# Attention over all keys: the context's scores are taken earlier and turned in a score bank, three query-tile score sets are made ahead instead of five, and two query tiles are turned inside the first iteration

## The chip, the cores and the metric

One Trainium2 chip, one core of it. Its engines are PE (TensorE: matrix products and transposes; its weight loads are PEld), DVE (VectorE), ACT (ScalarE), POOL (GpSimd) and SP (SyncE, which only issues transfers here). Each has its own queue of instructions and runs it in order; they wait for each other through semaphores. PE writes into eight PSUM banks, which ACT and DVE empty.

The metric is the device time of one execution in microseconds (us), the median of several; less is better. The kernel before takes 1534.35 us (three runs, 1534.03 to 1535.56).

## What is computed

Two layers of a diffusion backbone over 1024 latent tokens and 128 context tokens, 1024 features wide. The change lies in one part of layer 0, the grouped-query attention: 8 query heads share 2 key heads of 64 features. Cut to what matters:

```python
def block_attend(q, k, v):                       # q (B,KV,G,T,D); k, v (B,KV,S,D)
    s = einsum('bkgqd,bksd->bkgqs', qi, k) * scale
    p = softmax(s, axis=-1)
    return einsum('bkgqs,bksd->bkgqd', p, v)

qb = rmsnorm(to_heads(qb, HQ_B), g_q)            # then axial rope
k_all = concatenate([kb_pos, kv_ctx[0]], axis=2) # 1024 latent + 128 cached keys
hb = block_attend(qb, k_all, v_all)              # latent queries
```

The 128 context tokens attend to themselves alone, with the same heads; that is a small separate attention. What follows is `y = concat(ha, hb) * silu(z)` and the output projection.

## The kernel before

Tokens are nine tiles of 128 (0 to 7 latent, 8 context). A float32 operand is cut into a high and a low part, so that each product is two or three matmuls.

**Phase g** makes keys, values and queries. `gqa_q` (L848) runs twice, for the first and the last four query heads (g = 0, 1). For each tile i it multiplies the normalised input by the weights (`tok`, L381 to L383: 24 matmuls of 256 columns into a bank of the pair "pj"), applies norm and rope on ACT, DVE and POOL (`norm_rope`, tile nr), turns the result with two PE transposes (L106) into the bank "tr" (even i) or "ptr" (odd i), and cuts the turned tile into Q: for each half of the partitions ACT casts the high part (L875) and DVE subtracts it (L876). In the program the second half's cast waits for the first half's subtraction.

In the second run some **score sets** are made ahead (`early`): a set is one query tile with one pair of heads against the 1152 keys, in six score groups. A group is two matmuls of 384 columns (L907) into one of three banks "s", which DVE copies out with the running extreme (L908). After three groups (one head) ACT takes the exponential over 1152 columns (L914), DVE the reciprocal (L915), POOL the division in three pieces (L917). The order of all engines in phase g is made by a scheduler with estimated times.

**Phase gqa** (`gqa`, L955) works off 32 sets, two at a time: j is the pair of heads (0 to 3), i = 0, 2, 4, 6 the query tile pair. One iteration holds ten **turn steps** n = 0 to 9 (`gqa_turn`, L922), each with four PE transposes of probabilities (two in steps 4 and 9) into the banks tr, pj, ptr, pj in rotation, emptied into the tiles pt by ACT (L938), in steps 4 and 9 by DVE (L936). Between them stand the score groups of the next two sets, one after each step and two ahead (`steps`); then the **apply**, 36 matmuls of 256 columns (L947) into bank "o". PE's order here is that of the code (`manual_schedule`); the other engines follow the scheduler.

In iteration i = 6 of each j the **context tile** is attended to as well (`ctx_steps`, L1014): four small score matmuls (L1023) into two s banks, DVE's maximum (L1024), two exponentials on ACT (L1027), sum and reciprocal on DVE (L1028, L1029), division on POOL (L1030); then two transposes of the result into bank "tr" (L106, tr<-pt) and their copy; after the apply the product with the values (L1042).

For j >= 2 each iteration also cuts one block of the output weights: a transfer into a buffer "raw", ACT's high part (L114), POOL's low part wlo (L115). The **output projection** follows (L381 to L383 with yh, yl). Its tile 0 is loaded by SP (y<-yd) into a buffer raw that the last weight block has left, and is cut by ACT (yh) and DVE (yl).

Of the kernel before, what the change touches and what calls it, by code (L numbers as in the profile page):

```python
# [10 lines left out]
F32 = mybir.dt.float32  # L11
F32R = mybir.dt.float32r
AF = mybir.ActivationFunctionType
ALU = mybir.AluOpType
# [4 lines left out]
P = 128  # L19
# [7 lines left out]
DHB = 64  # L27
# [12 lines left out]
class Kern:  # L40
    def __init__(self, ctx, tc, a, dbg):
        self.tc, self.nc, self.a, self.dbg = tc, tc.nc, a, dbg
        mk = lambda n, **k: ctx.enter_context(tc.tile_pool(name=n, bufs=1, **k))
        self.cp = mk("const")
        self.up = mk("slots")
        self.wp = mk("stage")
        self.sp = mk("small")
        self.dp = mk("scratch", space=DRAM)
        self.pp = mk("psum", space=PSUM)
        self.uid = 0  # L50
        self.flip = 0
        self.turn = 0

    @contextmanager
    def phase(self, n, *tags):
# [794 lines left out]
    def gqa_q(self, h, g, w, Qs, early):  # L850

        nc = self.nc
        ahead = None
        rhs = lambda k: tuple(x[:, (k % 4) * 256 : (k % 4 + 1) * 256] for x in w[k // 4])
        Q = []
        for i in range(NT):
            if i == NT - 4:
                ahead = self.gqa_weights(2) if g == 0 else self.gqa_gate(0)
            if i in (0, 2, 4, 6, 8) and g:
                n = len(early)  # L860
                q0 = Qs[0][n // 2][:, n % 2]
                early.append([])
                for _ in self.gqa_scores([q0[:, hh] for hh in range(2)], 0, lambda s: self.u(s, n="pr"), early[-1]):
                    pass
            ps = self.tok(h, i, rhs, 256)
            q = self.norm_rope(ps, 4, 0, i)
            pt = self.ps(("tr", "ptr")[i % 2])[:, :256]
            for j in range(2):
                self.flipped(pt[:, j * P : (j + 1) * P], q[:, 2 * j : 2 * j + 2].rearrange("p a b -> p (a b)"))
            if i % 2 == 0:  # L870
                Q.append(self.u([P, 2, 4, P], F32R, n="Q"))
            for hh in range(2):
                x = pt[hh * DHB : (hh + 1) * DHB].rearrange("p (a b) -> p a b", b=P)
                hi, lo = (Q[-1][r * DHB : (r + 1) * DHB, i % 2, hh::2, :] for r in (g, 1 - g))
                nc.scalar.copy(hi, x)  # L875
                nc.vector.tensor_tensor(lo, x, hi.bitcast(F32), ALU.subtract)  # L876
        return Q, ahead

    def zb(self, h):
# [74 lines left out]
    def gqa(self, Q, gz, early, between):  # L954

        kv = lambda j: j // 2
        V = lambda t, j: t[..., kv(j) * DHB : (kv(j) + 1) * DHB]
        q = lambda j, i: [Q[kv(j)][i // 2][:, i % 2, 2 * (j % 2) + hh, :] for hh in range(2)]  # L960
        place = (lambda s: self.t("pr", 4, s)), (lambda s: self.u(s, n="pr"))
        todo = iter([(j, i) for j in range(4) for i in range(8)])

        def tiles(out):
            for j, i in itertools.islice(todo, 2):
                if early:
                    out.append(early.pop(0))
                else:
                    prs = []
                    yield from self.gqa_scores(q(j, i), kv(j), place[i % 2], prs)  # L970
                    out.append(prs)

        prs, banks = [], ("tr", "pj", "ptr", "pj")
        for _ in tiles(prs):
            pass
        for j in range(4):
            y = self.ytile()
            for i in range(0, 8, 2):
                if i % 4 == 0:
                    po = self.ps("o")  # L980
                nxt, pts = [], ([], [])
                steps = tiles(nxt)
                turns = self.gqa_turn(prs, pts, banks)
                if i == 6:
                    ctx = self.ctx_steps([self.gqa_terms(x, kv(j), [self.KstP[:, b] for b in range(4)]) for x in q(j, 8)], [V(self.VP, j)] * 2, self.pt)
                next(steps, None)
                next(steps, None)
                for n, _ in enumerate(turns):
                    if i == 6 and n == 1:
                        next(ctx)  # L990
                    else:
                        next(steps, None)
                    if i == 6 and n == 6:
                        next(ctx)
                for _ in steps:
                    pass
                self.gqa_apply(pts, V(self.V, j), po[:, i % 4 * P : (i % 4 + 2) * P])
                if i == 6:
                    cpo = next(ctx)
                prs = nxt  # L1000
                if j >= 2:
                    next(between, None)
                if i % 4:
                    self.put_y(4 + j, slice((i - 2) * P, (i + 2) * P), po, gz, y)
            self.put_y(4 + j, slice(8 * P, NT * P), cpo, gz, y)
            gz = self.gqa_gate(j + 1) if j < 3 else None
        return y
# [624 lines left out]
```

## Time and profile before

| | |
|---|---|
| median of three runs | 1534.35 us |
| the profiled execution, its own time | 1537.54 us |
| its span, first to last instruction | 1535.8 us |
| PE busy | 1493.2 us, 97% |
| DVE, ACT, POOL busy | 54%, 46%, 29% |
| mean granted clock of PE over the span | 0.995 |

A timeline row has the start, the time of one instruction or a run of equal ones, engine, line, what is written from what, the count, and in brackets the idle time ahead with what ended it. A row of waits says which engine and line waited for which, with total time, number of waits and the longest. [...]

### The profile page before, as it was taken

The numbers are of one execution on the slowest core, as the hardware profiler recorded it, in microseconds if no ns is written. First come the engines' busy times: TensorE is split into PE (matmuls) and PEld (weight loads), VectorE is DVE, ScalarE is ACT, GpSimd is POOL, SyncE is SP. The second block draws the span as 40 slices with busy tenths as digits, with TensorE's granted clock in tenths as the row PEclk, the third lists the DMA queues.
The fourth block names the chain that finished last, engine by engine and source line by source line (L and its number), as shares of the span: only waits on it lengthen the run. The fifth ranks groups of instructions, "written<-read, shape, count | busy, mean of one in ns | idle before, by whom it ended". The sixth has DMA issues, their size and how long they took to land.

```text
span 1535.8 us, 27072 instructions
## 1 busy us (share of the span) xinstructions
PE 1493.2 (97%) x10139; PEld 1375.7 (90%) x10139; DVE 825.7 (54%) x2387; ACT 712.5 (46%) x1767; POOL 448.6 (29%) x644
## 2 busy tenths in 40 slices
PE   7899999999999899999999999999999999999998
PEld 5799999999999888877888989999999999988786
DVE  5832888863468666665565352535344434445532
ACT  4533535262446667776444352535344434345411
POOL 0001202011146645675223241323133222233200
PEclk9999999999999999999999999999999999999999
DMA  9203447332310000112334222131213122125342
GB/s 378 76 15 140 179 146 248 125 121 75 111 48 29 16 32 24 44 64 68 135 114 138 70 65 74 36 106 34 85 38 103 32 79 71 54 90 163 106 132 82
DMA packets 73283, 143.80 MB, mean 94 GB/s; under 512 B 15736, under 2 KB 44608, under 8 KB 73152
## 3 DMA queue, kind: packets, MB, share of 16 engines
q1 hardware_dynamic: 68566, 126.91, 24.7%
q10 hardware_dynamic: 4586, 15.16, 2.7%
q8 instruction: 80, 1.31, 0.3%
q14 instruction: 51, 0.42, 0.1%
HBM read 115.47 MB, written 21.86 MB: 89 GB/s over the span
## 4 chain that ended last, share of the span: by engine, by line
PE 49%; DMA 1%; DVE 1%; ACT 1%; POOL 1%; issue 1%; DVEq 0%; POOLq 0%
PE pj L366 7%; PE pj L367 7%; PE pj L368 7%; PE pj L382 6%; PE pj L381 6%; PE pj L383 6%; PE o L1282 4%; PE s L1259 3%; PE ptr L106 2%; PE tr L106 2%; DMA y<-yd 1%; DMA raw<-in_w_out_dram 1%; POOL wlo L115 0%; PE o L947 0%; DVE sb L1265 0%
## 5 line engine op out<-in xcount | busy, mean ns | idle before, releaser
L366 PE MATMUL pj<-hh,whi 128*128 128x384 f32 x1168 | 400.2, 343 | 1.9 <-ACT qT L101 1.2
L367 PE MATMUL pj<-hl,whi 128*128 128x384 f32 x1168 | 397.0, 340 | 0.0
L368 PE MATMUL pj<-hh,wlo 128*128 128x384 f32 x1168 | 395.6, 339 | 0.4 <-DVE wlo L115 0.4
L366 PEld LDWEIGHTS pj<-hh,whi 128*128 128x128 f32 x1168 | 219.6, 188 | 5.6 <-ACT qT L101 1.8
L368 PEld LDWEIGHTS pj<-hh,wlo 128*128 128x128 f32 x1168 | 219.3, 188 | 1.6 <-DVE wlo L115 0.6
L367 PEld LDWEIGHTS pj<-hl,whi 128*128 128x128 f32 x1168 | 219.8, 188 | 1.1
L1269 POOL TENSOR_SCALAR sb<-sb,sm 128x512 f32<-128x512 f32 (+1 forms) x128 | 84.7, 667 | 249.3 <-DVE sm L1268 237.6
L115 POOL TENSOR_TENSOR wlo<-raw,whi 128x1024 fp32r<-128x1024 f32 x43 | 103.0, 2400 | 133.0 <-ACT whi L114 115.7
L917 POOL TENSOR_SCALAR pr<-pr,smg 128x384 f32<-128x384 f32 x192 | 109.3, 586 | 80.5 <-PE pj L106 41.2
L381 PE MATMUL pj<-whi,hh 128*128 128x256 f32 x432 | 122.6, 285 | 0.3 <-DVE nr L782 0.3
L382 PE MATMUL pj<-wlo,hh 128*128 128x256 f32 x432 | 122.7, 284 | 0.0
L383 PE MATMUL pj<-whi,hl 128*128 128x256 f32 x432 | 122.4, 284 | 0.0
L908 DVE CUSTOM_DVE_ANT_0 pr<-s,zero 128x384 f32<-128x384 f32 x192 | 103.4, 553 | 24.9 <-PE s L907 21.4
L381 PE MATMUL pj<-whi,yh 128*128 128x512 f32 x288 | 114.2, 396 | 1.5 <-DVE o L1077 1.5
L382 PE MATMUL pj<-wlo,yh 128*128 128x512 f32 x288 | 113.7, 395 | 0.0
L383 PE MATMUL pj<-whi,yl 128*128 128x512 f32 x288 | 113.3, 394 | 0.0
L1267 ACT ACTIVATE sb<-sb,sm 128x512 f32<-128x512 f32 (+1 forms) x128 | 88.9, 695 | 52.7 <-DVE sm L1265 48.8
L907 PE MATMUL s<-Kst,Q 128*128 128x384 f32 x384 | 107.6, 372 | 0.7 <-DVE smg L908 0.7
L253 DVE CUSTOM_DVE_ANT_0 mj<-wm,cb 128x512 f32<-128x512 f32 x128 | 89.3, 697 | 5.1 <-DMA wm<-in_w_modT_dram 2.8
L114 ACT CAST whi<-raw 128x1024 fp32r<-128x1024 f32 x77 | 79.7, 1045 | 19.9 <-DMA raw<-in_w_v_dram 6.9
L1265 DVE CUSTOM_DVE_ANT_1 sb<-s,bias 128x512 f32<-128x512 f32 (+1 forms) x112 | 72.9, 664 | 24.9 <-PE ptr L106 12.6
L381 PEld LDWEIGHTS pj<-whi,hh 128*128 128x128 f32 x432 | 81.3, 188 | 1.3 <-issue 0.5
(346 smaller groups left out, 2908.8 us busy)
## 6 DMA issues: line engine op xcount, KB each, us to landing
wm<-in_w_modT_dram SPq DMA_DIRECT2D x32, 512.0 KB, 4.8
raw<-in_w_c_dram SPq DMA_DIRECT2D x25, 512.0 KB, 3.6
raw<-in_w_ab_dram SPq DMA_DIRECT2D x20, 512.0 KB, 3.5
e<-rbd ACTq DMA_DIRECT2D x12, 768.0 KB, 7.4
bias<-in_na_bias_dram SPq DMA_DIRECT2D x16, 576.0 KB, 4.1
wm<-in_w_mod_dram SPq DMA_DIRECT2D x16, 512.0 KB, 9.8
raw<-in_w_out_dram SPq DMA_DIRECT2D x16, 512.0 KB, 3.5
y<-yd SPq DMA_DIRECT2D x18, 448.0 KB, 3.4
```

The source lines that it names most:

```text
L115: (eng_lo or nc.gpsimd).tensor_tensor(lo, src, hi.bitcast(F32), ALU.subtract)
L253: nc.vector.tensor_tensor_reduce(junk, w[:, b, :], cb[:, r, :], 1.0, 0.0, ALU.mult, ALU.add, mp[:, hf, q // 4, 2 * (q % 4) + b, r : r + 1])
L366: nc.tensor.matmul(ps[:, :CW], a, hh, start=k == 0, stop=False)
L367: nc.tensor.matmul(ps[:, :CW], a, hl, start=False, stop=False)
L368: nc.tensor.matmul(ps[:, :CW], b, hh, start=False, stop=k == KB - 1)
L381: nc.tensor.matmul(ps[:, :width], hh, a, start=k == 0, stop=False)
L382: nc.tensor.matmul(ps[:, :width], hh, b, start=False, stop=False)
L383: nc.tensor.matmul(ps[:, :width], hl, a, start=False, stop=k == KB - 1)
L907: nc.tensor.matmul(s[:, :CW], x, y, start=part == 0, stop=part == 1)
L908: nc.vector.tensor_tensor_reduce(pr[:, c, :], s[:, :CW], zero, -1.0, -NEG, ALU.add, ALU.min, m3[:, c : c + 1])
L917: nc.gpsimd.tensor_scalar(pr[:, c, :], pr[:, c, :], r, 0.5, ALU.mult, ALU.mult)
L1267: nc.scalar.activation(x, x, AF.Exp, bias=nm, scale=-1.0, accum_out=r)
```

## The change

Three edits. First, the sets made ahead in phase g are three instead of five, at tiles 1, 3 and 5. Second, in the second run of `gqa_q` the turning of tiles 7 and 8 is put off: it is kept as a function, called in the first iteration of phase gqa behind turn steps 5 and 7. Third, the context tile's scores are put into iteration i = 4 behind step 7, in the place of a score group; its transposes come behind step 5 of iteration i = 6, ahead of the group there, and go to an s bank instead of tr.

```diff
-            if i in (0, 2, 4, 6, 8) and g:
+            if i in (1, 3, 5) and g:
...
-            pt = self.ps(("tr", "ptr")[i % 2])[:, :256]
...
+            def turned(i=i, q=q, Qt=Q[-1]):
+                pt = self.ps(("tr", "ptr")[i % 2])[:, :256]
...
+            if g and i in (7, 8):
+                self.turned.append(turned)
+            else:
+                turned()
...
-                if i == 6:
-                    ctx = self.ctx_steps([self.gqa_terms(x, kv(j), [self.KstP[:, b] for b in range(4)]) for x in q(j, 8)], [V(self.VP, j)] * 2, self.pt)
+                if i == 4:
+                    ctx = self.ctx_steps([self.gqa_terms(x, kv(j), [self.KstP[:, b] for b in range(4)]) for x in q(j, 8)], [V(self.VP, j)] * 2, self.pt, banks=("s", "s"))
...
-                    if i == 6 and n == 1:
+                    if (j, i, n) in ((0, 0, 5), (0, 0, 7)):
+                        self.turned.pop(0)()
+                    if i == 4 and n == 7 or i == 6 and n == 5:
                         next(ctx)
-                    else:
+                    if (i, n) != (4, 7):
                         next(steps, None)
-                    if i == 6 and n == 6:
-                        next(ctx)
```

Eight lines are added ahead, so that L106 becomes L107, L875 L878, L907 L915, L914 L922, L938 L946, L947 L955, L1023 L1031 and L1030 L1038.

**Place 1, the seam of phases g and gqa.** PE before, from the turning of tile 7 (nr_5712) to that of tile 8 (nr_5802) and the first turn steps (pr into ptr, pj); the s rows are the last sets made ahead:

```order
L106 MATMUL ptr_5726<-cc,nr_5712 128x128 x2
L907 MATMUL s_5757<-Kst_4302,Q_4980 128x384
L907 MATMUL s_5757<-Kst_4304,Q_4980 128x384
L907 MATMUL s_5761<-Kst_4302,Q_4980 128x384
L907 MATMUL s_5761<-Kst_4304,Q_4980 128x384
L907 MATMUL s_5765<-Kst_4302,Q_4980 128x384
L907 MATMUL s_5765<-Kst_4304,Q_4980 128x384
L106 MATMUL tr_5816<-cc,nr_5802 128x128 x2
L106 MATMUL ptr_5845<-cc,pr_5183 128x128
L106 MATMUL ptr_5845<-cc,pr_5320 128x128
L106 MATMUL ptr_5845<-cc,pr_5183 128x128
```

Now tiles 7 (nr_5668) and 8 (nr_5707) stand among the turn steps 5 to 8 of the first iteration; PE:

```order
L107 MATMUL ptr_5809<-cc,pr_5389 128x128
L107 MATMUL ptr_5815<-cc,nr_5668 128x128 x2
L107 MATMUL pj_5822<-cc,pr_5252 128x128
L107 MATMUL pj_5822<-cc,pr_5389 128x128
L107 MATMUL pj_5822<-cc,pr_5252 128x128
L107 MATMUL pj_5822<-cc,pr_5389 128x128
L107 MATMUL tr_5828<-cc,pr_5252 128x128
L107 MATMUL tr_5828<-cc,pr_5389 128x128
L107 MATMUL tr_5828<-cc,pr_5252 128x128
L107 MATMUL tr_5828<-cc,pr_5389 128x128
L107 MATMUL tr_5834<-cc,nr_5707 128x128 x2
```

Tile 7 goes into the bank ptr right behind a turn step that filled it, tile 8 into tr likewise. ACT there, from the second exponential of set 2 (pr_5528) to the copy that frees tr for tile 8:

```order
L922 ACTIVATE pr_5528,smg_5544<-pr_5528,smg_5542 128x1152
L946 COPY pt_5726<-pj_5747 128x512
L878 CAST Q_5635<-tr_5636 64x2x128
L946 COPY pt_5726<-ptr_5765 128x512
L922 ACTIVATE pr_5737,smg_5759<-pr_5737,smg_5757 128x1152
L946 COPY pt_5727<-pj_5777 128x512
L946 COPY pt_5727<-tr_5787 128x512
L946 COPY pt_5728<-ptr_5809 128x512
L922 ACTIVATE pr_5771,smg_5799<-pr_5771,smg_5797 128x1152
L878 CAST Q_5635<-ptr_5815 64x2x128
L946 COPY pt_5729<-pj_5822 128x512
L946 COPY pt_5729<-tr_5828 128x512
```

Two exponentials of the set now made in this iteration (pr_5737, pr_5771) have come in between the copies.

**Place 2, the context tile of j = 0.** PE before, in iteration 6 from a score group to the turning of the context's probabilities (pt_5830) and on:

```order
L907 MATMUL s_6301<-Kst_4302,Q_4794 128x384
L907 MATMUL s_6301<-Kst_4304,Q_4794 128x384
L106 MATMUL tr_6305<-cc,pt_5830 128x128 x2
L106 MATMUL ptr_6309<-cc,pr_6068 128x128
L106 MATMUL ptr_6309<-cc,pr_6146 128x128
```

Now PE has the context's scores in the end of iteration 4 (KstP is the context's keys):

```order
L107 MATMUL tr_6140<-cc,pr_5981 128x128
L1031 MATMUL s_6147<-KstP,Q_5175 128x128 x2
L1031 MATMUL s_6151<-KstP,Q_5175 128x128 x2
L107 MATMUL pj_6161<-cc,pr_5903 128x128
L107 MATMUL pj_6161<-cc,pr_5981 128x128
L107 MATMUL pj_6161<-cc,pr_5903 128x128
L107 MATMUL pj_6161<-cc,pr_5981 128x128
L915 MATMUL s_6169<-Kst_4302,Q_5082 128x384
L915 MATMUL s_6169<-Kst_4304,Q_5082 128x384
L107 MATMUL ptr_6173<-cc,pr_5903 128x128
L107 MATMUL ptr_6173<-cc,pr_5981 128x128
L915 MATMUL s_6177<-Kst_4302,Q_5082 128x384
```

The scores have moved up by most of an iteration; the third score group behind them (s_6177) waits in the program for the first of the context's two exponentials.

**Place 3, the end of the phase.** POOL before, from the division of the last set but one to the context's division (L1030):

```order
L917 TENSOR_SCALAR pr_8184<-pr_8184,smg_8212 128x384 x3
L115 TENSOR_TENSOR wlo_8277<-raw_8274,whi_8276 128x1024
L917 TENSOR_SCALAR pr_8224<-pr_8224,smg_8250 128x384 x3
L115 TENSOR_TENSOR wlo_8379<-raw_8376,whi_8378 128x1024
L1030 TENSOR_TENSOR pt_5830<-pt_5830,sm_8301 128x256
```

POOL now:

```order
L925 TENSOR_SCALAR pr_8184<-pr_8184,smg_8212 128x384 x3
L1038 TENSOR_TENSOR pt_5726<-pt_5726,sm_8233 128x256
L116 TENSOR_TENSOR wlo_8292<-raw_8289,whi_8291 128x1024
L925 TENSOR_SCALAR pr_8245<-pr_8245,smg_8265 128x384 x3
L116 TENSOR_TENSOR wlo_8379<-raw_8376,whi_8378 128x1024
```

The context's division stands ahead of the last two weight blocks instead of behind them.

## Rows read from the trace of the kernel before

**Rows 1.** The page: busy time, share of the span, instructions.
```profile
PE 1493.2 (97%) x10139; PEld 1375.7 (90%) x10139; DVE 825.7 (54%) x2387; ACT 712.5 (46%) x1767; POOL 448.6 (29%) x644
```

**Rows 2.** Waits of PE from 400 to 720 us: total, times, longest.
```profile
PE tr L106 <- POOL pt L1030: 6.2, 4, 2.2
PE ptr L106 <- DVE Q L876: 1.9, 1, 1.9
PE tr L106 <- DVE Q L876: 0.9, 1, 0.9
...
PE s L907 <- DVE smg L908: 0.7, 1, 0.7
```

**Rows 3.** Timeline of PE at the seam of phases g and gqa.
```profile
514.61 0.28 PE L383 MATMUL pj<-whi,hl 128*128 128x256 f32 x1
...
519.51 0.44 PE L106 MATMUL tr<-cc,nr 128*128 128x128 f32 x2 [0.50 <-POOL nr L784]
521.87 1.09 PE L106 MATMUL ptr<-cc,pr 128*128 128x128 f32 x4 [1.92 <-DVE Q L876]
...
528.90 4.11 PE L947 MATMUL o<-pt,V 128*64 128x256 f32 x36
```

**Rows 4.** Windows there: length; busy PE, PEld, DVE, ACT, POOL; granted clock; DMA.
```profile
520.00:521.00 1.00, 0.00 (x0) 0.00 (x0) 1.00 (x5) 0.97 (x2) 1.00 (x3) 0.96 0.00 0
521.00:522.00 1.00, 0.13 (x1) 0.16 (x2) 0.91 (x5) 0.95 (x4) 0.14 (x1) 0.50 0.00 0
...
527.00:528.00 1.00, 1.00 (x8) 1.00 (x7) 0.00 (x0) 0.67 (x2) 0.00 (x0) 0.63 0.00 0
```

**Rows 5.** Timeline of PE in the next two iterations.
```profile
539.27 4.20 PE L947 MATMUL o<-pt,V 128*64 128x256 f32 x36
...
551.77 4.11 PE L947 MATMUL o<-pt,V 128*64 128x256 f32 x36
```

**Rows 6.** Timeline of ACT in iteration 4 of j = 0.
```profile
549.12 1.26 ACT L914 ACTIVATE pr<-pr,smg 128x1152 f32<-128x1152 f32 x1
...
550.37 0.57 ACT L938 COPY pt<-pj 128x512 f32<-128x512 f32 x1
550.84 0.60 ACT L938 COPY pt<-tr 128x512 f32<-128x512 f32 x1
```

**Rows 7.** Groups of ACT by line and shape, 455 to 730 us: busy, mean ns.
```profile
L775 ACT ACTIVATE nr<-pj 128x64 f32<-128x64 f32 x68 | 14.4, 221 | 9.6 <-PE pj L383 8.5 <-POOL sm L134 0.9
...
L875 ACT CAST Q<-ptr 64x256 fp32r<-64x256 f32 x16 | 5.9, 367 | 4.5 <-DVE Q L876 2.4 <-PE ptr L106 1.9
...
L1027 ACT ACTIVATE pt<-s,sm 128x128 f32<-128x128 f32 x8 | 2.9, 363 | 0.0
```

**Rows 8.** Timeline of PE at the end of phase gqa.
```profile
711.85 0.66 PE L106 MATMUL pj<-cc,pr 128*128 128x128 f32 x4
...
717.74 0.44 PE L106 MATMUL tr<-cc,pt 128*128 128x128 f32 x2 [2.20 <-POOL pt L1030]
...
719.44 5.50 PE L947 MATMUL o<-pt,V 128*64 128x256 f32 x36
...
725.09 0.50 PE L381 MATMUL pj<-whi,yh 128*128 128x512 f32 x1
```

**Rows 9.** Timeline of POOL there.
```profile
709.02 1.71 POOL L917 TENSOR_SCALAR pr<-pr,smg 128x384 f32<-128x384 f32 x3 [0.43 <-DVE smg L912]
...
714.72 2.40 POOL L115 TENSOR_TENSOR wlo<-raw,whi 128x1024 fp32r<-128x1024 f32 x1
717.09 0.60 POOL L1030 TENSOR_TENSOR pt<-pt,sm 128x256 f32<-128x256 f32 x1
```

**Rows 10.** Timeline of SP's queue there.
```profile
717.14 0.38 SPq L1056 DMA_DIRECT2D y<-yd  x1
```

**Rows 11.** Timeline of ACT there.
```profile
720.71 0.94 ACT L114 CAST yh<-y 128x896 fp32r<-128x896 f32 x1 [0.93 <-DMA y<-yd]
```

**Rows 12.** Window there, columns as in rows 4.
```profile
718.00:719.00 1.00, 1.00 (x11) 1.00 (x10) 0.42 (x1) 0.29 (x1) 0.00 (x0) 0.94 0.58 145
```

More of the change, by code (lines that the diff above doesn't have):

```diff
@@ L52, in __init__ @@
         self.turn = 0
+        self.turned = []
     @contextmanager
@@ L866, in gqa_q @@
             q = self.norm_rope(ps, 4, 0, i)
-            pt = self.ps(("tr", "ptr")[i % 2])[:, :256]
-            for j in range(2):
-                self.flipped(pt[:, j * P : (j + 1) * P], q[:, 2 * j : 2 * j + 2].rearrange("p a b -> p (a b)"))
             if i % 2 == 0:
                 Q.append(self.u([P, 2, 4, P], F32R, n="Q"))
[L872 to L876, printed above, removed]
+            def turned(i=i, q=q, Qt=Q[-1]):
+                pt = self.ps(("tr", "ptr")[i % 2])[:, :256]
+                for j in range(2):
+                    self.flipped(pt[:, j * P : (j + 1) * P], q[:, 2 * j : 2 * j + 2].rearrange("p a b -> p (a b)"))
+                for hh in range(2):
+                    x = pt[hh * DHB : (hh + 1) * DHB].rearrange("p (a b) -> p a b", b=P)
+                    hi, lo = (Qt[r * DHB : (r + 1) * DHB, i % 2, hh::2, :] for r in (g, 1 - g))
+                    nc.scalar.copy(hi, x)
+                    nc.vector.tensor_tensor(lo, x, hi.bitcast(F32), ALU.subtract)
+            if g and i in (7, 8):
+                self.turned.append(turned)
+            else:
+                turned()
         return Q, ahead
```

## The prediction

> **What bounds the kernel now.** I read the page's busy times first: PE is busy for 97% of the span [rows 1], so only PE's queue sets the end. A moved instruction can save no PE work; it can save idle time of PE or time at the half clock. The list of PE's waits is read next, over the stretch that the change touches, 400 to 720 us [rows 2]. The largest item is the context's transposes waiting for POOL's division (L1030): 6.2 us in four waits, one for each pair of heads, the longest 2.2, so 4.0 in the other three. Three smaller ones (1.9 and 0.9 on DVE's low part of Q, 0.7 on the score copies) lie in one place, the seam between phases g and gqa.
>
> Then the timelines of these places. At the seam PE has the last projection matmul at 514.61 (T0 from here) and the first apply at 528.90 [rows 3]: 14.3 us. [...] At the end of gqa the wait of 2.20 ends at 717.74 [rows 8], the clock leaves the full level in 718 to 719 [rows 12], and the apply there takes 5.50 [rows 8] instead of the 4.11 of the first one [rows 3]. An apply during a low clock thus costs 1.4 us more.
>
> Times below are made against the profiled execution, 1537.54 us with a span of 1535.8 (1.7 around it); it is 3.2 above the median of 1534.35. The gain is taken over to the median.
>
> **1. Six score groups moved from phase g into iteration 2.** Six of the early groups go. Iteration 2 of j = 0 goes from 6 groups to 12. From the end of the first apply (528.90 + 4.11) to the second (539.27) are 6.3 us with six groups; from that apply's end (543.47) to the third (551.77) are 8.3 with twelve [rows 3, 5]. So a group costs PE 0.34 us, and six cost 2.0 here and save 2.0 in phase g, where they also filled PE's time. I take 0. Were they covering waits of PE on norm and rope, as much as those 2.0 would be lost; nothing excludes a gain of the size of the 0.7 on the score copies [rows 2].
>
> **2. The seam.** The work between T0 and the apply is the same on PE: six groups, ten turn steps, three turnings of Q. At full speed that is 6.3 us (iteration 2 has the same ten steps and six groups) plus three turnings of at most 0.44 [rows 3], 7.6. So the gain is at most 14.3 - 7.6 = 6.7, and the waits decide. The waits of 1.92 and 0.86 on Q's low parts go: tile 8 no longer stands ahead of the turn steps. What is late next is ACT, because two exponentials of the set that is now made here stand between its copies. By the new order ACT has, from T0 to the copy that frees tr for tile 8: four squares at 0.22, three Q casts at 0.37 [rows 7], three exponentials at 1.25 with the reading of the sum and seven copies at 0.47 [rows 6]: 0.9 + 1.1 + 3.75 + 3.3 = 9.05. With 0.4 before the first (T0's matmul must end) and 0.5 for exponentials that wait for DVE's minimum, T0 + 9.9. Tile 7 goes into bank ptr right behind a turn step that filled it, and so waits for the copy of that step: about 1.4 us on PE. Tile 8 in tr waits likewise, about 1.6, until T0 + 10. Queued behind each of them on PE are all later turn steps and the apply. Then tile 8, two turn steps and the last group, 1.1: apply at T0 + 11.1, against 14.3: 3.2 gained at full clock.
>
> The clock takes part of it back. Before, it fell after the 0.50 and inside the 1.92 [rows 3, 4]; now two waits of 1.4 and 1.6 stand within about four us, and I take it that it falls behind them. It then hits the apply, 1.4 by [rows 3, 8], and about 0.4 of turn steps. Net 1.4. The bounds are 0 (ACT and the clock eat all) and 6.7.
>
> [...]
> [...]
>
> **3. The context tile, j = 0 to 2.** Scores go into iteration 4 and the transposes come most of an iteration later, so POOL's 0.6 us division [rows 9] is long done: 4.0 us of waits removed [rows 2]. Added: the context's two score banks are held until ACT has run its exponentials, which are 0.36 each [rows 7] but stand behind copies and perhaps a long exponential; the third score group behind the context's scores waits in the program for the first of them. No row of before shows that wait. It is between 0 (ACT free) and 1.25 + 0.36 [rows 6, 7] = 1.6; I take 0.35 each, nearer to zero because a third s bank, a turn step and a group lie between. Net 3.0, bounds 4.0 and -0.8 (4.0 less three of 1.6). On POOL the context's division moves ahead of work of the next sets, 0.6 that the sets' divisions can carry where they are not the last thing waited for.
>
> **4. The end, j = 3.** Here the wait of 2.20 and the low clock under the apply go, 3.6 and some 0.6 of turn steps: PE would be done at about 720.7 instead of 724.9 (719.44 + 5.50 [rows 8]). But the output projection needs yh and yl of its tile 0. Their transfer goes out when the last wlo has freed the raw buffer (wlo 714.72 + 2.40, issue at 717.14 [rows 9, 10]), and ACT's cast starts 3.57 later, at 720.71 [rows 11]. The new order puts the 0.6 division ahead of the last two wlo, and the context's scores take a group's place in iteration 4, so that the last group comes one group (0.34) later: last wlo done at about 718.1, cast from 721.7 to 722.65. On SP the load of x, which used to go out behind y, now stands ahead of it and is not held by the wlo; that makes y's landing no later, and perhaps 0.5 earlier. So the projection starts at about 722.8 instead of 725.09: 2.3, taken as 2.2. PE waits here for about 1.7 at a new place. Bounds: 0 (y comes as late as 725) and 4.2.
>
> **Sum.** 0 + 1.4 + 3.0 + 2.2 = 6.6, taken as 6.7 with the 0.1 to 0.2 of PE restarts that go with the removed waits: 1537.54 becomes 1530.8, and the median 1527.6.
>
> **The rivals.**
>
> *B, the clock holds at the seam and POOL is not later at the end.* The seam then gives 3.2 and the end about 3.2: 1.8 + 1.0 more, a gain of 9.5, 1524.9. For: no single wait there is as long as the 1.92 that went ahead of the fall. Against: there are two of them close together.
>
> *C, the clock falls at the new wait ahead of the output projection.* Before, it fell behind waits of at most 2.2 [rows 8, 12], and 1.7 is close to it. Its first four us of work at half speed cost 2: gain 4.7, 1529.7. [...]
>
> *D, both ends give their gain back.* ACT ends the seam where it ended before, and y arrives with the old end. For: both chains are ACT's and POOL's, and PE only follows. Then the three context waits alone remain, 3.0: 1531.3.
>
> *E, slower: banks in iteration 4.* Each j has two of the three s banks held behind a long exponential (1.25 + 0.47 + 0.36 = 2.1 [rows 6, 7]), and the turned context in an s bank until its copy, 1.6 more: up to 3.7 for each of four, 14.8 in all, against 7.6 gained (1.4, 4.0 and 2.2): 7.2 slower, 1541.6. It decides from 1.9 us of new PE wait for each j on. Against: PE's groups can go on in the third bank.
>
> *F, the scheduler undoes it.* The new order shows all three edits on PE, so little: 1534.
>
> **How the numbers follow.** The forecast has 0.47, B 0.18, C 0.17, D 0.10, E 0.05, F 0.03. The forecast's own range, by the clock at the seam and the context's new waits, is 1525.5 to 1530. The range over all takes in B's time and most of C and D: 1524.0 to 1532.0. A measurement can tell about 0.2% (3.1 us) from no change: faster is below 1531.3. That is the forecast, B, nearly all of C and half of D less what their spread puts beyond: 0.80; the same 0.15; slower 0.05, E.
>
> **What the profile of the changed kernel would show.** Right: PE's waits on POOL's context division are gone; at the seam PE waits in ptr and tr for ACT's copies, tile 7's and tile 8's turnings carrying 1.4 and 1.6; the apply starts 11 to 12 us behind T0, with a window near 0.50 around it; a small wait of s on ACT once in each j; y goes out at about 718 on the old time line, and the first matmul of the projection waits for the cast. Iteration 2 is 2 us longer. Wrong in step 2: no clock below 1.0 near the first apply (B), or the apply not before T0 + 13.5 (D). Wrong in step 3: s waits of a us or more in iteration 4, or a context copy that holds the score groups (E). Wrong in step 4: the clock down in the first microseconds of the output projection (C), or its start less than 1 us earlier against the last turn steps (D).

## The result, and the profile after

The changed kernel takes 1526.81 us (median of five runs, 1525.72 to 1527.66) against 1534.35: 7.5 us less, a ratio of 0.9946 with a 95% interval of 0.9935 to 0.9956. The profiled execution took 1527.66 with a span of 1525.9.

The waits of PE from 395 to 715 us come first, as [rows 2] for before (engine, line, what it waited for; total, times, longest):

```profile
PE tr L107 <- ACT pt L946: 1.4, 1, 1.4
PE s L915 <- ACT pt L1035: 1.1, 4, 0.3
PE ptr L107 <- ACT pt L946: 1.0, 1, 1.0
PE pj L107 <- DVE nr L783: 0.7, 1, 0.7
PE tr L107 <- DVE Q L879: 0.4, 1, 0.4
```

The 6.2 us on POOL's division are gone; in their place are four waits of 0.3 on the context's exponential (L1035). The 1.92 and the 0.86 on Q's low part are gone too; ACT's copies (L946) have taken their place at the seam. There the timeline of PE reads, against [rows 3]:

```profile
512.29 0.28 PE L384 MATMUL pj<-whi,hl 128*128 128x256 f32 x1
...
515.72 0.63 PE L107 MATMUL pj<-cc,pr 128*128 128x128 f32 x4 [0.66 <-DVE nr L783]
...
519.71 0.41 PE L107 MATMUL ptr<-cc,nr 128*128 128x128 f32 x2 [0.95 <-ACT pt L946]
...
522.44 0.41 PE L107 MATMUL tr<-cc,nr 128*128 128x128 f32 x2 [1.45 <-ACT pt L946]
...
523.57 4.11 PE L955 MATMUL o<-pt,V 128*64 128x256 f32 x36
```

From T0 (512.29) to the first apply are 11.28 us instead of 14.30, and the apply takes 4.11. The windows, with the columns of [rows 4] and the granted clock as a share of full speed, show where most of this comes from: the clock stays at 1.00 even in the window in which PE does nothing.

```profile
521.00:522.00 1.00, 0.00 (x0) 0.00 (x0) 0.42 (x2) 0.97 (x3) 0.90 (x2) 1.00 0.00 0
522.00:523.00 1.00, 0.56 (x5) 0.59 (x6) 0.28 (x1) 0.78 (x3) 0.81 (x2) 1.00 0.00 0
```

For the context tile of j = 0, PE's timeline has the scores in iteration 4, the one new wait, and the turning in an s bank without a wait:

```profile
546.48 0.64 PE L1031 MATMUL s<-KstP,Q 128*128 128x128 f32 x4
...
548.45 0.96 PE L915 MATMUL s<-Kst,Q 128*128 128x384 f32 x4 [0.30 <-ACT pt L1035]
...
558.34 0.38 PE L107 MATMUL s<-cc,pt 128*128 128x128 f32 x2
```

At the end of the phase, against [rows 8], PE has the last iteration, the apply at full clock, and a wait for the cast of y:

```profile
706.23 0.66 PE L107 MATMUL pj<-cc,pr 128*128 128x128 f32 x4
...
710.64 4.11 PE L955 MATMUL o<-pt,V 128*64 128x256 f32 x36
...
716.30 0.50 PE L382 MATMUL pj<-whi,yh 128*128 128x512 f32 x1 [1.33 <-ACT yh L115]
```

Its cause in POOL, in SP's queue and in ACT, against [rows 9 to 11]: the last wlo ends at 711.82, y goes out at 711.85, the cast starts at 715.31.

```profile
709.45 2.37 POOL L116 TENSOR_TENSOR wlo<-raw,whi 128x1024 fp32r<-128x1024 f32 x1
```
```profile
711.85 11.51 SPq L1064 DMA_DIRECT2D y<-yd  x3
```
```profile
715.31 0.94 ACT L115 CAST yh<-y 128x896 fp32r<-128x896 f32 x1 [4.08 <-DMA y<-yd]
```

The window of that wait still has the full clock:

```profile
715.00:716.00 1.00, 0.00 (x0) 0.00 (x0) 0.71 (x2) 0.69 (x1) 0.00 (x0) 1.00 0.00 0
```

All kernels are compared by the same marks on PE's timeline, in the profile of each (us). "g" runs from one fixed instruction of PE in phase g (at 425.46 in before) to T0; "seam" from T0 to the first apply; "it. 2" from there to the second apply; "it. 4" to the third; "j loop" from there to the apply of iteration 4 of j = 3; "end" from there to the first matmul of the output projection. The last two columns are the longest wait of PE at the seam and about how long the granted clock was low around it. Each row is one execution, and not always one near its kernel's median: early_only's (1531.85) is the fastest of its eleven, turn_only's (1539.43) the slowest of its eleven, the changed kernel's the slowest of its five, and seam_only's (1534.69) lies 3.0 above the median.

| kernel | g | seam | it. 2 | it. 4 | j loop | end | sum | wait | low |
|---|---|---|---|---|---|---|---|---|---|
| before | 89.14 | 14.30 | 10.36 | 12.51 | 156.04 | 17.27 | 299.62 | 1.92 | 7 |
| changed | 86.96 | 11.28 | 12.39 | 13.38 | 152.86 | 14.10 | 290.97 | 1.45 | 0 |
| ctx_only | 89.12 | 15.34 | 10.59 | 13.48 | 153.00 | 14.31 | 295.84 | 1.92 | 10 |
| seam_only | 86.96 | 11.90 | 13.23 | 12.42 | 156.00 | 17.25 | 297.76 | 1.45 | 3 |
| early_only | 86.99 | 12.79 | 12.48 | 12.42 | 155.94 | 17.18 | 297.80 | 2.40 | 3 |
| turn_only | 89.10 | 15.25 | 12.07 | 12.52 | 155.93 | 17.28 | 302.15 | 2.12 | 10 |
| hold | 86.96 | 14.05 | 14.05 | 13.37 | 152.85 | 14.82 | 296.10 | 2.69 | 3 |
| flip | 87.01 | 14.33 | 14.76 | 13.37 | 152.85 | 14.27 | 296.59 | 2.73 | 7 |
| dcast | 86.99 | 10.60 | 12.39 | 13.38 | 152.85 | 14.26 | 290.47 | 0.95 | 0 |
| tail | 86.96 | 11.27 | 12.38 | 12.94 | 151.53 | 14.25 | 289.33 | 1.5 | 0 |
| div | 87.00 | 11.28 | 12.36 | 13.38 | 152.88 | 13.78 | 290.70 | 1.5 | 0 |
| wlo | 86.96 | 11.26 | 12.39 | 13.38 | 152.85 | 13.70 | 290.54 | 1.5 | 0 |
| all4 | 86.99 | 10.61 | 12.39 | 12.95 | 151.69 | 13.52 | 288.15 | 0.97 | 0 |

The whole change is 8.65 us in these marks: 2.2 in phase g and 3.0 at the seam gained, 2.0 lost in iteration 2, and 5.5 gained in the rest by the context's edit. The two profiles differ by 9.9; the other 1.2 lie outside the marks, 0.1 ahead of them and 1.1 behind, in stretches that the change does not touch.

### The profile page after: what moved, and what is told of

It is laid out like the page before. It is cut to its first block, busy times and chain, and to the rows that moved or that the text cites. A ratio compares the mean times of both kernels' runs of the same rounds, so it can differ in the third digit from the quotient of the medians.

```text
span 1525.9 us, 27070 instructions
## 1 busy us (share of the span) xinstructions
PE 1489.1 (98%) x10139; PEld 1370.8 (90%) x10139; DVE 828.0 (54%) x2387; ACT 711.9 (47%) x1767; POOL 449.3 (29%) x644
## 4 chain that ended last, share of the span: by engine, by line
PE 49%; DMA 1%; DVE 1%; ACT 1%; POOL 1%; issue 0%; DVEq 0%; POOLq 0%; ACTq 0%
PE pj L367 7%; PE pj L368 7%; PE pj L369 7%; PE pj L383 6%; PE pj L382 6%; PE pj L384 6%; PE o L1290 4%; PE s L1267 3%; PE ptr L107 2%; PE tr L107 2%; DMA y<-yd 1%; POOL wlo L116 1%; DMA raw<-in_w_out_dram 0%; DVE sb L1273 0%; POOL pr L925 0%
## 5 line engine op out<-in xcount | busy, mean ns | idle before, releaser
L915 PE MATMUL s<-Kst,Q 128*128 128x384 f32 x384 | 107.8, 372 | 1.1 <-ACT pt L1035 1.1
```

Source lines behind the costliest of these rows:

```text
L915: nc.tensor.matmul(s[:, :CW], x, y, start=part == 0, stop=part == 1)
```

## The experiments

**The kernel before, again.** No edit.

> The kernel before once more, to read the granted clock of each of its runs. Theory: the low clock at the seam (6.8 us) and at the end (3.4 us) is in every run, since it follows waits that are in every run; then all runs stand within 1 us of 1534.3 and show a mean clock near 0.996. Rival: it falls in some runs only; then the runs spread by 2 us or more with the mean clock between 0.995 and 0.999, and the gain by medians (7.5) is smaller than by the two profiles (9.9) because the profile of before had more of it than the median run.

Median 1535.69 (eleven runs, 1534.42 to 1537.02), ratio to before 0.9997, interval 0.9989 to 1.0006. The theory's "within 1 us of 1534.3" missed: the runs spread by 2.6 us, as the rival said. But the mean granted clock was 0.995 or 0.996 in each of the eleven runs, and the profile has the same marks as before's to 0.1 us (seam 14.37, end 17.28), with 1534.58 instead of 1537.54. So the low clock at both places is in both profiles, and the eleven mean clocks agree with its being in every run; what spreads the runs is not shown. The 3 us by which the first profile stood above this one lie elsewhere: 1.1 ahead of phase g's mark and 1.9 behind the start of the projection. Single medians of one kernel in two series differ by 1.3 us (1534.35 and 1535.64), so ratios are used below.

**The two halves apart.** ctx_only has only the third edit (context's scores in iteration 4, turned in a score bank); seam_only has the first two.

```diff
-                if i == 6:
+                if i == 4:
...
-                    if i == 6 and n == 1:
+                    if i == 4 and n == 7 or i == 6 and n == 5:
...
```

> Only the context's edit (scores in iteration 4, turned in a score bank in iteration 6). Theory (each place has its own gain): j = 0 to 2 give 3.0 and the end 2.2 to 2.4, so 5.3 in all, 1529.0, with the seam as before and its low clock there. Rival: the end's gain hangs on the earlier seam; then 3.0 alone, 1531.3.

> The three early sets and the late turning together, without the context's edit. Theory: the profiles of the whole change put 3.0 at the seam and 0.2 in the moved groups, so 1531.2, with no low clock ahead of the first apply and with the low clock at the end as before. Rival (before's median run loses less at the seam than its profile): 1.5 to 2, 1532.6.

ctx_only: 1531.72, ratio 0.9978 (0.9969 to 0.9986), 3.4 us. seam_only: 1531.67, ratio 0.9977 (0.9969 to 0.9986), 3.5 us. Together 0.9955, against 0.9946 measured for the whole change; the halves add up within the intervals. seam_only's gain is what its theory expected (3.15). ctx_only's median alone would fit its rival (3.0), but by the marks it does what the theory says: from the second apply on it gains 5.0 (185.82 to 180.79), the same as the whole change but for 0.4. The end's gain does not need the earlier seam. Its median misses the expected 1529.0 by 2.7; 1.3 of that is the series, in which before has 1535.64. Most of the rest stands at the seam, where nothing was edited: its waits there are those of before to 0.01 us (0.74, 0.51, 1.92, 0.86), but in its profile the clock stays low into the first apply. Windows of ctx_only at the seam, columns as in [rows 4]:

```profile
518.00:519.00 1.00, 0.32 (x2) 0.09 (x2) 0.97 (x5) 0.91 (x2) 1.00 (x3) 0.80 0.00 0
...
527.00:528.00 1.00, 1.00 (x7) 1.00 (x5) 0.00 (x0) 0.59 (x1) 0.00 (x0) 0.50 0.00 0
528.00:529.00 1.00, 1.00 (x6) 0.45 (x6) 0.42 (x1) 0.59 (x1) 0.00 (x0) 0.58 0.00 0
```

That is some 10 us instead of 7 and costs 1.2 to 1.3 (seam and iteration 2 together, against the two profiles of before). Its timed runs have a mean clock of 0.995 to 0.997, no higher than before's, although the low clock at the end is gone from the profile; so the longer low stretch is likely in most of them, which the profile of one run cannot prove. seam_only shows the other side of it. Its waits at the seam are those of the changed kernel (0.64, 0.42, 0.96, 1.45), and yet in its profile the clock falls behind the 1.45:

```profile
523.00:524.00 1.00, 0.81 (x5) 0.84 (x6) 0.43 (x1) 0.64 (x3) 0.56 (x1) 0.66 0.00 0
524.00:525.00 1.00, 1.00 (x7) 0.67 (x6) 0.42 (x1) 0.51 (x2) 0.00 (x0) 0.50 0.00 0
```

The mean clock of this profiled run is 0.997; in nine of the eleven timed runs it is 0.998 or 0.999, as in the changed kernel. So the fall need not be in most of its runs, and its 1.86 by the marks (299.62 to 297.76) stands below the 3.5 by the ratio.

**The seam's two edits apart.**

```diff
-            if i in (0, 2, 4, 6, 8) and g:
+            if i in (1, 3, 5) and g:
```

The kernel early_only has this edit alone; turn_only has the late turning of tiles 7 and 8 alone.

> Only the three early sets at tiles 1, 3 and 5; tiles 7 and 8 are turned where they were. Theory: moving groups is worth nothing by itself, and the wait of 1.92 for Q's low part stays, so 1534.3 within 1 us, with the low clock at the seam. Rival 1: two exponentials that come between the copies make the seam longer by 1 to 2.5, up to 1537. Rival 2: it is this edit that gives the seam's 3.0, 1531.3.

> Only the late turning of tiles 7 and 8; the five early sets stay. Theory (the seam's gain is the removed waits of 1.92 and 0.86 on Q's low part, and the early sets only shift six groups): from the last projection matmul to the second apply 24.7 us become 22 to 23, a gain of 2 to 3, 1533 against a before of 1535.6. Rival (the turning gains only where score groups of the first iteration fill PE between the turn steps): PE waits for ACT's copies as long as it waited for Q, gain under 0.5.

early_only: 1533.57, ratio 0.9991 (0.9983 to 1.0000), a gain of 1.4 that its interval just allows to be none; its theory (1534.3 within 1 us) holds, and neither rival does. turn_only: 1537.04, ratio 1.0010 (1.0002 to 1.0019), 1.5 slower. The theory of turn_only is wrong, and its rival is nearer: PE waits for ACT's copies longer than it had waited for Q. Alone, each edit gives little or costs, and together they gain 3.5. In early_only the tile is still turned ahead of the turn steps and PE's wait for Q's low part is even longer, 2.40:

```profile
515.91 1.02 PE L106 MATMUL ptr<-cc,pr 128*128 128x128 f32 x4 [2.40 <-DVE Q L876]
```

In turn_only the waits move from Q to ACT's copies and are no shorter. ACT's timeline (top) and PE's show it: ACT stands idle for 1.34 ahead of the exponential at 520.63, until DVE has the set's minimum, and the copies of banks that PE has long filled stand behind it in ACT's queue.

```profile
520.63 1.25 ACT L922 ACTIVATE pr<-pr,smg 128x1152 f32<-128x1152 f32 x1 [1.34 <-DVE smg L920]
...
522.00 0.59 ACT L946 COPY pt<-pj 128x512 f32<-128x512 f32 x1
```
```profile
522.64 0.44 PE L107 MATMUL pj<-cc,pr 128*128 128x128 f32 x2 [1.46 <-ACT pt L946]
...
525.91 0.66 PE L107 MATMUL ptr<-cc,nr 128*128 128x128 f32 x2 [2.12 <-ACT pt L946]
```

With the set spread over the turn steps (the early edit), the first copies run from T0 + 3.0 (515.28) instead of T0 + 6.2 (522.00), between the exponentials. The early edit changes the number of sets and the tiles at which they are made; which of the two counts was not tested.

**A longer wait at the seam.** hold repeats one cast of tile 7 on ACT.

```diff
-                    nc.scalar.copy(hi, x)
+                    for _ in range(5 if g and i == 7 and hh == 0 else 1):
+                        nc.scalar.copy(hi, x)
```

> The changed kernel with ACT's first cast of tile 7 done five times over (the same values), 4 x 0.37 = 1.5 us more in ACT's queue at the seam. Theory: it goes straight into PE's wait ahead of tile 8's turning, 1.45 becomes 2.9, and with a wait of that length the clock falls to 0.50 as it did in before behind 1.92; the first apply then takes 5.5 or more and comes 3 to 4.5 us later in all: 1530 to 1531. Rival: the clock does not hang on the length of this wait; then 1.5 later alone, 1528.3, with a granted clock of 1.00 at the seam.

1532.63, ratio 0.9980 (0.9971 to 0.9989): 5.2 us above the changed kernel by the ratios, more than expected. The place was wrong; the clock fell as the theory said. The repeated casts were set between the copies, so they hold tile 7's bank ptr, and it is turn step 9 that waits for it, 2.69. Then the clock falls, and the apply takes 5.79 instead of 4.11. PE's timeline, and a window:

```profile
527.04 0.44 PE L107 MATMUL ptr<-cc,pr 128*128 128x128 f32 x2 [2.69 <-DVE Q L880]
527.41 5.79 PE L956 MATMUL o<-pt,V 128*64 128x256 f32 x36
```
```profile
528.00:529.00 1.00, 1.00 (x8) 0.62 (x6) 0.00 (x0) 0.00 (x0) 0.00 (x0) 0.50 0.08 16
```

The seam is 2.8 longer and iteration 2 another 1.7, which is the clock's price on one apply; together 4.4, inside the 3 to 4.5 expected. The other 0.7 stand in the end: y goes out at the same place, its cast starts 0.7 later, and PE waits 2.06 for it. At that wait the clock holds: it is 1.00 in each window from 720 to 726.

```profile
722.50 0.50 PE L382 MATMUL pj<-whi,yh 128*128 128x512 f32 x1 [2.06 <-ACT yh L115]
```

The mean clock of the eleven timed runs is 0.996 to 0.998 against 0.998 to 0.999 for the changed kernel. hold adds one long wait and with it lengthens the sum of the waits at the seam; it does not tell which of the two the clock follows.

**The banks swapped.** flip turns tile 7 in tr and tile 8 in ptr.

```diff
-                pt = self.ps(("tr", "ptr")[i % 2])[:, :256]
+                pt = self.ps(("tr", "ptr")[(i + (g and i > 6)) % 2])[:, :256]
```

> The changed kernel with the two banks swapped for the late turnings: tile 7 goes into tr behind step 5, which filled ptr, and tile 8 into ptr behind step 7, which filled tr; so neither needs the copy of the step just ahead. Theory (the waits of 1.0 and 1.45 come from the bank chosen, but ACT's queue ends the seam): the two waits go, but later steps wait for ACT's casts in the same banks, and the apply comes 0 to 0.5 earlier: seam 10.8 to 11.3, 1526.5. Rival (the banks are the cost): 1.5 to 2.4 earlier, seam 9 to 9.8, 1524.8.

1532.28, ratio 0.9979 (0.9970 to 0.9988): 5.1 worse than the changed kernel, against both the theory and its rival. Tile 7's wait falls from 0.95 to 0.47, but now a turned tile stands in the very bank that the next turn step needs, and it leaves that bank only after two casts on ACT and two subtractions on DVE:

```profile
521.63 0.63 PE L107 MATMUL tr<-cc,pr 128*128 128x128 f32 x4 [2.73 <-DVE Q L879]
...
524.87 0.66 PE L107 MATMUL ptr<-cc,pr 128*128 128x128 f32 x2 [1.96 <-DVE Q L879]
```

The clock falls with it. The bank that looks worst, the one just filled, was the better one here (a seam of 11.28 against 14.33): a turn step's bank is emptied by one copy, a tile's by a chain of four instructions on two engines (in the changed kernel's rows a copy of 0.59 against two casts of 0.36 to 0.37 and two subtractions of 0.42 to 0.43).

**The casts on DVE.** dcast takes the four casts of tiles 7 and 8 from ACT.

```diff
-                    nc.scalar.copy(hi, x)
+                    (nc.vector.tensor_copy if g and i > 6 else nc.scalar.copy)(hi, x)
```

> The changed kernel with the four casts of tiles 7 and 8 on DVE instead of ACT, 4 x 0.37 = 1.5 us less in ACT's queue at the seam. Theory (ACT's queue ends the seam): one cast stands ahead of the copy that tile 8 waits for and two more ahead of the last copies, so the apply comes 0.4 to 0.8 earlier, seam 10.5 to 10.9, 1526.2. Rival (PE's own work and the banks end it): seam 11.3 as before, 1526.8.

Median 1527.04, ratio 0.9944 (0.9932 to 0.9957), by the medians not to be told from the changed kernel. By the marks the theory holds: the seam falls to 10.60 (all4, with the same edit: 10.61), where the four profiles of kernels that leave it as in the changed one have 11.26 to 11.28, while PE's work is the same, and tile 8's wait from 1.45 to 0.93.

```profile
521.41 0.41 PE L107 MATMUL tr<-cc,nr 128*128 128x128 f32 x2 [0.93 <-ACT pt L946]
```

**The context's scores last.** tail puts them behind the last score group of iteration 4.

```diff
-                    if i == 4 and n == 7 or i == 6 and n == 5:
+                    if i == 6 and n == 5:
                         next(ctx)
-                    if (i, n) != (4, 7):
-                        next(steps, None)
+                    next(steps, None)
                 for _ in steps:
                     pass
+                if i == 4:
+                    next(ctx)
```

> The changed kernel with the context's scores behind the last score group of iteration 4, ahead of the apply, in place of step 7. Theory: no score group waits for the context's exponential any more, so the four waits of 0.3 (1.1 us in all) go; the last group comes 0.34 earlier, and the end with it: 1.1 to 1.5 less than the changed kernel, 1525.5. Rival: the exponentials of the context now stand behind the last long exponential in ACT and hold the s banks into the next iteration, the wait reappears there; same as the changed kernel, 1526.8.

1526.22, ratio 0.9935 (0.9923 to 0.9948). The marks give 1.6 less than the changed kernel: 0.44 for each of the four iterations 4, of which 0.30 is the wait and 0.14 stands in no row of waits. No wait of a score group on the context's exponential is left. The end, which runs from the apply of iteration 4, gains nothing of the 0.34: it is 14.25, with a wait for y of 1.51. The kernels that leave the end as in the changed one have 14.10 to 14.31 and waits of 1.33 to 1.55 (hold alone 14.82 and 2.06), so this wait has not grown by the edit:

```profile
714.98 0.50 PE L382 MATMUL pj<-whi,yh 128*128 128x512 f32 x1 [1.51 <-ACT yh L115]
```

**What ends the end.** div computes the context's division on DVE; wlo the low part of the last weight block on DVE.

```diff
-        nc.gpsimd.tensor_tensor(pr, pr, r[:, :2, None].to_broadcast([P, 2, P]), ALU.mult)
+        (nc.gpsimd if po is not None else nc.vector).tensor_tensor(pr, pr, r[:, :2, None].to_broadcast([P, 2, P]), ALU.mult)
```
```diff
-        return self.weights(self.a["w_out"][l, j], ("", "lo")[j % 2] if l else "")
+        return self.weights(self.a["w_out"][l, j], ("", "lo")[j % 2] if l else ("", "lo")[j == KB - 1])
```

> The changed kernel with the context's division on DVE instead of POOL. Theory (the start of the output projection hangs on POOL's last wlo, which frees the buffer of y): POOL has 0.6 less ahead of it, the transfer of y goes out 0.6 earlier against the last turn steps, PE's wait of 1.33 ahead of the projection becomes 0.7: 0.6 less than the changed kernel, 1526.2. Rival: the last wlo waits for ACT's high part or for the scores' division, not for POOL's own queue; y goes out at the same time and nothing changes.

> The changed kernel with the low part of the last weight block on DVE instead of POOL. Theory (the projection waits for y, y for the buffer that the last wlo frees, and that wlo for POOL's queue): the wlo ends 2 to 3 us earlier than POOL's, y comes under the last apply and PE's wait of 1.33 ahead of the projection goes: 1.0 to 1.4 less than the changed kernel, 1525.5. Rival: DVE's score copies and turn-step copies are held up by it, PE waits for them in the last iteration as much: 1526.8.

div: 1527.09, ratio 0.9943 (0.9930 to 0.9957); wlo: 1527.23, ratio 0.9947 (0.9934 to 0.9959). Neither can be told from the changed kernel by its median. By the marks the end falls by 0.3 and by 0.4, to 13.78 and 13.70, below all kernels that leave the changed kernel's end as it is (14.10 to 14.31, and 14.82 in hold). That agrees with POOL's queue setting it, but each gives half or less of what was expected. In div the transfer goes out 5.18 behind the first turn step of the last iteration (705.31 to 710.49) instead of 5.62, so 0.44 of the 0.6. In wlo the wait for y is gone, and another has come: POOL's division of the last set, for which the turn steps wait, takes 2.73 beside the DVE's wlo, where it took 1.73. POOL, DVE and PE:

```profile
706.47 2.73 POOL L925 TENSOR_SCALAR pr<-pr,smg 128x384 f32<-128x384 f32 x3
```
```profile
705.17 2.40 DVE L116 TENSOR_TENSOR wlo<-raw,whi 128x1024 fp32r<-128x1024 f32 x1 [0.77 <-ACT whi L115]
```
```profile
708.13 0.55 PE L107 MATMUL tr<-cc,pr 128*128 128x128 f32 x3 [0.89 <-POOL pr L925]
...
714.61 0.50 PE L382 MATMUL pj<-whi,yh 128*128 128x512 f32 x1
```

**The four together.** all4 has the edits of dcast, tail, div and wlo.

> The changed kernel with four edits together: casts of tiles 7 and 8 on DVE, the context's scores behind the last score group of iteration 4, the context's division on DVE, the last weight block's low part on DVE. Theory (each edit has a place of its own): from the last projection matmul to the output projection the changed kernel takes 204.0; less 0.7 at the seam, 1.5 in the context's iterations, and 0.7 to 1.0 at the end (no wait for y, and the scores' division on POOL starts 0.6 earlier, so that its slower run beside DVE costs no wait) are 200.8 to 201.1, a median of 1523.7 against 1526.8. Rival (the DVE edits get in each other's way in the last iteration): the end stays at 14.1 and the gain is 2.0, 1524.8.

1526.02, ratio 0.9939 (0.9926 to 0.9953). The marks give 2.8 less than the changed kernel (288.15 against 290.97), almost what the theory expects (201.15 from T0 to the projection, for 200.8 to 201.1). One step of it failed: POOL's division (2.65, where it took 1.73 in the changed kernel) does cost a wait, and the end gives 0.6 for the 0.7 to 1.0. PE:

```profile
707.39 0.55 PE L107 MATMUL tr<-cc,pr 128*128 128x128 f32 x3 [0.71 <-POOL pr L925]
```

The ratios show 1.1 of the 2.8, and the intervals of the two ratios overlap, so a version that beats the changed kernel is not shown. Its profile has the clock low for some 3 us each at two places far from all edits, and four of its five runs have a mean clock of 0.997 or 0.998. Whether the edits have anything to do with that stays open.

## Why the prediction was right, and where it was not

The forecast was 1527.6 and the range 1524.0 to 1532.0; 1526.81 was measured. Step by step:

**1, the moved groups.** Taken as 0. Phase g became 2.18 shorter and iteration 2 became 2.03 longer: 0.15 gained. Right.

**2, the seam.** The gain was taken as 1.4 and measured as 3.0. The queue of ACT was right almost to the row: the copy that frees tr was put at T0 + 9.9 to 10, and tile 8 is turned at T0 + 10.15; the apply was put at T0 + 11.1 at full clock and came at 11.28. One term of that sum is not seen: ACT has no wait there for DVE's minimum, for which 0.5 was put; the instructions themselves took that much more together. Waits of 1.4 and 1.6 were forecast, 0.95 and 1.45 came. What failed is the sentence "I take it that it falls behind them": the clock held, and the 1.8 that were taken off for it were not lost. So at the seam rival B happened; its other half, an end without a later POOL, did not. The waits alone fell little, from 4.0 to 3.5 us (0.66, 0.41, 0.95 and 1.45); most of the 3.0, some 2.5, is the clock. Over all profiles here it fell at the seam in each kernel whose longest wait was 1.92 or more (before, its repetition, ctx_only, turn_only, early_only, hold, flip), and held in each whose longest was at most 1.5, but for seam_only. So taking the fall as the likely case was wrong here, but a kernel that stands at 1.45 has no assurance, and the other kernel with the same waits shows it. That the longest wait is what counts is read off these profiles, one per kernel; it is not shown.

The prediction says of the 1.92 and the 0.86 that they go because "tile 8 no longer stands ahead of the turn steps". By turn_only that is only half of it: without the set spread over the turn steps, ACT's copies come late and as much time is lost.

**3, the context, j = 0 to 2.** 3.0 forecast, 3.18 measured in the j loop (156.04 to 152.86). The new wait was taken as 0.35 and came as 0.30 in each j; in tail, which has no such wait, iteration 4 is 0.44 shorter. Rival E, score banks held for 2 to 4 us, did not happen: PE's waits there were 0.27 to 0.30, and the turned context held up no score group. That the third bank is the reason, as the prediction says, was not tested.

**4, the end.** 2.2 forecast. The end fell by 3.17, of which 0.87 is the context's scores and their wait that went into iteration 4 (12.51 to 13.38): 2.3 in all. Both parts of the reason are seen: the low clock under the apply is gone (5.50 to 4.11), and PE waits for the cast of y at the place named, 1.33 for the 1.7. That the sum comes out so close is in part luck, since two parts of it are off and cancel. Counted from the apply of iteration 2 of j = 3 (695.42 in before, 688.84 now), POOL's last wlo ends 1.3 later, for the 1.0 that was put: iteration 4 is 0.96 longer there, not one group of 0.34, and behind its apply the wlo is 0.3 later (9.62 against 9.30). From the wlo's end to the projection it took 4.5, for the 4.7 that was put. Rival C, the clock falling at this wait, did not happen; no run shows the four us at half speed in its price, and in before the low clock at this place lasted some 3.4 us. div and wlo bear out that y's chain through POOL ends the phase: with an earlier POOL the projection starts earlier.

**The sum.** 6.7 forecast; 8.65 by the two profiles in the touched stretch; 7.5 by the medians and 8.3 by the ratio. No run shows the 0.1 to 0.2 of PE restarts in the forecast's sum; the nearest to it is tail's 0.14 in each iteration 4 beyond the wait of 0.30. Most of the difference, 1.6 of the 2.0 by the profiles, is the clock at the seam. That the forecast of 1527.6 comes within 0.8 of the median is in part luck: the stretch gave 2.0 more than forecast, and the medians show 1.1 less than the stretch.

## What to carry to other kernels

Price a wait of PE twice: as idle time, and as a possible low clock under the work behind it, here up to 2.4 us on an apply (flip's first took 6.51 instead of 4.11), and 1.4 or 1.7 in before and hold. When a tile must pass through a bank of a rotation, count the instructions that empty the bank, not how recently it was filled (flip was 5.1 worse). When two edits share a place, try each alone: here one cost 1.5, one gained about 1.4, and both together gained 3.5.

## What the runs showed of the hardware

Equal waits did not give equal clocks. Before and ctx_only have the same waits at the seam to 0.01 us, and the clock was low for about 7 and about 10 us; the changed kernel and seam_only have the same waits within 0.02, and the clock held in one and fell in the other. Nor did one length divide the cases at both places: at the seam the clock fell at a longest wait of 1.92, and at the end of the phase it held at 2.06 (hold), while it fell in all five profiles in which PE waits there for POOL's division, 2.18 to 2.22.

Some instructions of DVE and POOL took longer beside a wlo of the other engine. A cast on DVE of 128 x 128 took 2.27 us in the changed kernel while POOL's wlo ran, and 0.21 in wlo and all4, where it came right behind a wlo on DVE, with a score division of POOL under way. In all4 the context's division, 0.57 us on DVE in iteration 4 of j = 0, took 2.33 at the end, beside POOL's wlo. DVE in the changed kernel, then DVE and POOL in all4:

```profile
705.61 2.27 DVE L113 CAST yh<-y 128x128 fp32r<-128x128 f32 x1
```
```profile
703.31 2.33 DVE L1039 TENSOR_TENSOR pt<-pt,sm 128x256 f32<-128x256 f32 x1
```
```profile
702.98 2.38 POOL L116 TENSOR_TENSOR wlo<-raw,whi 128x1024 fp32r<-128x1024 f32 x1
```

In all4 the DVE instruction begins 0.33 behind POOL's and ends 0.3 behind its end; in the changed kernel POOL's wlo ran from 705.41 to 707.79, and the cast began at 705.61 and ended at 707.88. In wlo it was POOL's division that took 2.73 for 1.73, begun at 706.47 while DVE's wlo ran from 705.17 to 707.57. In each of these three pairs the instruction that began later took longer; what held it is not shown.
